# Empty steps, pinned evacuations and two moved units in a gated hybrid decoder layer

## The chip, the cores and the metric

The kernel runs on one core of one Trainium2 chip. The core has a TensorE (PE, matmuls; its weight loads are shown apart as PEld), a VectorE (DVE), a ScalarE (ACT), a GpSimd (POOL) and a SyncE (SP); each works off its own queue in order, and they wait for each other by semaphores. The metric is the device time of one execution in microseconds; of several runs the median is taken.

## The reference

One decoder layer on 256 tokens of width 2048, in float32 (shapes and small helpers left out):

```
h = rmsnorm(x, pre_norm_g)
proj = h @ w_in                       # 2048 x 18448
a_q, a_k, a_v, a_g, a_lr, b_q, b_k, b_v, b_g, m_a, m_b = split(proj)
gk  = log_sigmoid(a_lr @ gla_gk_w2 + gla_gk_b) / 16
o_a = gla_chunked(a_q, a_k, a_v, gk)  # gated linear attention, 4 heads
y_a = (rmsnorm(o_a) * silu(a_g)) @ w_branch_a
o_b = diff_attention(b_q, b_k, b_v, lam)   # softmax - lam * softmax, 16 heads
y_b = (rmsnorm(o_b) * (1 - lam_init) * silu(b_g)) @ w_branch_b
merged = sigmoid(m_a) * y_a + sigmoid(m_b) * y_b
out = x + rmsnorm(merged @ w_out, post_norm_g)
```

## The kernel before

**Weights stream, in units.** All products with the weight matrices are made in units of 128 x 1024 weights. For each unit ScalarE copies the raw weights to a rounded `hi` (line 314, in the sets 273), VectorE subtracts to get `lo` (315, in the sets 274), and TensorE multiplies `hi` with both parts of the other operand and `lo` with the first part. A streamed unit of the v, ag, m, y and o weights is 12 matmuls of 512 columns or fewer (line 480), one of the dq and dk weights 16 (lines 501 and 503). `raw`, `hi` and `lo` have three buffers each; a raw buffer holds two units and is loaded on SP's queue (line 293).

**Sets.** Seven further pieces of the product (`SETS`: the heads' dv and bg, and most merge gates) are made by a seven-product block scheme (`PRODUCTS`) instead of eight. Each set has 28 units of 6 matmuls (line 673). Some of its weights are combined by adding transfers on POOL's queue into `chain` tiles (lines 217 and 218), some by VectorE (231, 236), and one product reads plain weights through a `raw` buffer (267).

**One written order.** `schedule()` lists all units of the streams and the sets in the order in which TensorE takes them. `mixed(n, keys)` spreads the next n set units evenly among the units of those keys, `alone(n)` puts n set units in a row. `take(key)` hands out the next unit; it also writes the copies of units up to `AHEAD` = 4 ahead.

**Side work as generators.** Everything else is written by generators in the list `tasks`: the linear attention's scores (`gla_scores`) and outputs (`gla_out`), the splits of q and k of a pair of heads (`diff_split`), the differential attention (`diff_attention`), fetches, and the last joining of the branches (`joined`, `turned`, `turn`). `pump(n)` steps the first n tasks once, up to their next `yield`; it is called after units of the streams and after every second set unit. `tc.issue_after(latest[0])` orders the TensorE instructions of a step behind the latest matmul written; instructions of the other engines have no such bound, and the scheduler that fills the queues may place them earlier when their inputs are ready. `tc.keep_in_program_order` pins an instruction to its written place against that. Flags in `done` order the tasks among themselves: `diff_scores` of a pair is written only when its `split` flag is set, and a pair's weighing only when its set is done.

**The places that the change touches.**

- `gla_out(hf, gates)`: for two heads the products with the values (462), the norm (901 to 904), the gated product into `ua` on VectorE (907), then a `yield`; then for four columns the transpositions of `ua` (916), their evacuation by `split_out` (513 on ScalarE, 514 on VectorE) and stores. The first half runs during ag2, where `fast[0]` is set and `pump` is called after every unit.
- `diff_split`: copies and differences for a pair's q2, kh and kl (954 to 959). `diff_heads` puts it at the head of `tasks` after a pair's four channel groups.
- `diff_attention`: per head scores (978, 979, 983, 989), weights (995 to 999), transposition (1004), weighing with the values (1010 to 1012), norm and gated product (1020 to 1027), and per pair of heads transpositions (1055) and `split_out`.
- `turn(g)`: for each quarter g of the columns eight transpositions of the merged tile (1175), then, one or two steps later, two evacuations to `mh` and `ml` by `split_out`. `mh` and `ml` are the operands of the last product, o0 to o3. The quarters 0 to 2 are turned during y12 and y13, quarter 3 during o0.
- `fetch_a`: fetches the eight `oah` and `oal` tiles during m12 and m13, pinned on SP's queue; y00 to y03 use them.

Of the kernel before, what the change touches and what calls it, by code (L numbers as in the profile page):

```python
# [10 lines left out]
AF = mybir.ActivationFunctionType  # L11
# [19 lines left out]
def chunk_plan():  # L31

    plan = []
    at = 0
    for g, n in enumerate(VG):
        if g == 0:
            plan.append(("v0", "two", "w_in", [(6144, RANK), (2048, 2 * n - RANK)]))
            at = 2 * n - RANK
        elif g > 1:
            plan.append((f"v{g}", "tok", "w_in", [(2048 + at, n)]))  # L40
            at += n
    for hf in range(2):
        for name, base in (("k", 1024), ("q", 0)):
            for c in range(4):
                plan.append((f"{name}{hf}{c}", "chan", "w_in", [(base + 512 * hf + P * c, P)]))
    for g in range(4):
        plan.append((f"ag{g}", "tok", "w_in", [(4096 + 512 * g, 512)]))
    o = 6144 + RANK

    def heads(g):  # L50
        plan.append((f"dv{g}", "tok", "w_in", [(o + 4096 + 512 * g, 512)]))
        plan.append((f"bg{g}", "tok", "w_in", [(o + 6144 + 512 * g, 512)]))
        for pair in range(2):
            for n, name in enumerate(("dq", "dk")):
                for c in (2 * pair, 2 * pair + 1):
                    plan.append((f"{name}{g}{c}", "chan", "w_in", [(o + 2048 * n + 512 * g + P * c, P)]))

    def gate(br, g):
        plan.append((f"m{br}{g}", "tok", "w_in", [(o + 8192 + 2048 * br + 512 * g, 512)]))

    def branch(br, g):
        plan.append((f"y{br}{g}", "tok", ("w_branch_a", "w_branch_b")[br], [(512 * g, 512)]))

    for g in range(4):
        heads(g)
    for br, g in ((1, 2), (1, 3), (1, 0), (1, 1), (0, 0), (0, 1), (0, 2), (0, 3)):
        gate(br, g)
    for br in range(2):
        for g in range(4):
            branch(br, g)  # L70
    for g in range(4):
        plan.append((f"o{g}", "tok", "w_out", [(512 * g, 512)]))
    return plan
# [6 lines left out]
def schedule():  # L80

    kinds = {key: kind for key, kind, _, _ in chunk_plan()}
    steps = []
    blocks = [(i, n) for i in range(len(SETS)) for n in range(SLOTS * 4)]

    def regular(*keys):
        steps.extend((key, n) for key in keys for n in range(units(kinds[key])))

    def mixed(n, *keys):
        at = len(steps)  # L90
        regular(*keys)
        r = steps[at:]
        del steps[at:]
        for i, step in enumerate(r):
            steps.extend(blocks[: (i + 1) * n // len(r) - i * n // len(r)])
            del blocks[: (i + 1) * n // len(r) - i * n // len(r)]
            steps.append(step)

    def channels(g):
        return [key for key in kinds if key[:2] in ("dq", "dk") and key[2] == str(g)]  # L100

    order = [key for key, _, _, _ in chunk_plan()]
    def alone(n):
        steps.extend(blocks[:n])
        del blocks[:n]

    regular(*order[: order.index("v4")])
    mixed(SLOTS * 4, *order[order.index("v4") : order.index("ag0")])
    regular("ag0", "ag1")
    mixed(5, "ag2")  # L110
    mixed(8, "ag3")
    mixed(15, *channels(0))
    mixed(19, *channels(1))
    mixed(20, *channels(2))
    mixed(20, *channels(3))
    mixed(18, "m12", "m13")
    mixed(43, *(f"y0{g}" for g in range(4)))
    alone(4)
    mixed(16, "y10", "y11")
    regular("y12", "y13", *(f"o{g}" for g in range(4)))  # L120
    assert not blocks
    return steps
# [28 lines left out]
def hybrid_kernel(ctx: ExitStack, tc, xt, xn, preg, postg, w, w2, gkb, glag, lamv, diffg, ident_d, causal_d, lmask_d, out):  # L151
    nc = tc.nc
    pe, act, dve, pool, sp = nc.tensor, nc.scalar, nc.vector, nc.gpsimd, nc.sync
# [298 lines left out]
    fast = [False]  # L452
# [56 lines left out]
        act.activation(t, bank, AF.Tanh, scale=half_rstd[:, b : b + 1])  # L509
        dve.scalar_tensor_tensor(out=dst, in0=t, scalar=1.0, in1=bank, op0=ALU.add, op1=ALU.mult)  # L510

    def split_out(bank, hi, lo, gain):
        act.activation(hi, bank, AF.Copy, scale=gain)
        dve.scalar_tensor_tensor(out=lo, in0=bank, scalar=gain, in1=f32(hi), op0=ALU.mult, op1=ALU.subtract)


# [253 lines left out]
    for g, n in enumerate(VG[2:]):  # L770
        banks = token_major(f"v{g + 2}", n, x_ops, 2)
# [114 lines left out]
    def gla_out(hf, gates):  # L886
        og = []
        while f"scores{hf}" not in done:
            yield
        fetch_values(2 * hf + 1)  # L890
        for h in range(2):
            (ah, al), xh_, xl_ = att[hf], vh[2 * hf + h], vl[2 * hf + h]
            banks = [ps("bg"), ps("bg")]
            trio = lambda i, b: ((ah[:, i, h, :], xh_[:, b, :]), (ah[:, i, h, :], xl_[:, b, :]), (al[:, i, h, :], xh_[:, b, :]))
            product(banks[0], trio(0, 0), True, True)
            product(banks[1], trio(2, 0), True, False)
            product(banks[1], trio(1, 1), False, True)
            ssq = sm([P, 2], "gssq")
            junk = sm([P, 512], "junk", BF16, bufs=1)
            for b in range(2):  # L900
                act.activation(junk, banks[b], AF.Square, accum_out=ssq[:, b : b + 1])
            dve.scalar_tensor_tensor(out=ssq, in0=ssq, scalar=1.0 / 512.0, in1=gla_eps, op0=ALU.mult, op1=ALU.add)
            rsqrt(ssq, ssq)
            dve.tensor_tensor(out=ssq, in0=ssq, in1=half_rstd, op=ALU.mult)
            o = gates[h]
            for b in range(2):
                dve.scalar_tensor_tensor(out=o[:, b, :], in0=banks[b], scalar=ssq[:, b : b + 1], in1=o[:, b, :], op0=ALU.mult, op1=ALU.mult)
            og.append(o)
            yield
        for j in range(4):  # L910
            if j % 2 == 0:
                oah[2 * hf + j // 2], oal[2 * hf + j // 2] = u([P, 2, 2, S], "oah", F32R), u([P, 2, 2, S], "oal", F32R)
            bank = ps("bg")
            for h in range(2):
                for b in range(2):
                    pe.transpose(bank[:, P * (2 * h + b) : P * (2 * h + b) + P], og[h][:, b, P * j : P * j + P], ident)
            i = 2 * hf + j // 2
            hi = oah[i][:, j % 2].rearrange("p h t -> p (h t)")
            lo = oal[i][:, j % 2].rearrange("p h t -> p (h t)")
            split_out(bank, hi, lo, glag_s[:, j : j + 1])  # L920
            if j % 2:
                pool.dma_start(oah_far[i], f32(oah[i]))
                pool.dma_start(oal_far[i], f32(oal[i]))
                yield
        done.add(f"out{hf}")
# [7 lines left out]
    for g in range(4):  # L933
# [3 lines left out]
        banks = token_major(f"ag{g}", 512, x_ops)  # L937
# [11 lines left out]
    obl_far = [away([P, 4, S], "obl_far") for _ in range(4)]  # L949

    def diff_split(g, pair, tq, tk, q2, kh, kl):
        for m in range(2):
            own, other = slice(64 * m, 64 * m + 64), slice(64 - 64 * m, P - 64 * m)
            act.activation(q2[own, m], tq[own], AF.Copy)
            dve.tensor_tensor(out=q2[other, m], in0=tq[own], in1=f32(q2[own, m]), op=ALU.subtract)
            act.activation(kh[own, m], tk[own], AF.Copy)
            act.activation(kh[other, m], tk[own], AF.Copy)
            dve.tensor_tensor(out=kl[own, m], in0=tk[own], in1=f32(kh[own, m]), op=ALU.subtract)
            pool.memset(f32(kl[other, m]), 0.0)
        yield  # L960
        yield
        done.add(f"split{g}{pair}")
        yield
# [169 lines left out]
    for g in (2, 3):  # L1133
        banks = token_major(f"m1{g}", 512, x_ops, 2)
# [4 lines left out]
    for g in range(4):  # L1139
        if g == 3:  # L1140
            tasks.append(fetch_b())
        banks = token_major(f"y0{g}", 512, a_ops)
# [24 lines left out]
    def turn(g):  # L1167

        banks = []
        for i in range(2):  # L1170
            bank = ps("bg")
            for j in range(2):
                for b in range(2):
                    c = P * (2 * i + j)
                    pe.transpose(bank[:, P * (2 * j + b) : P * (2 * j + b) + P], both[g][:, b, c : c + P], ident)  # L1175
            banks.append(bank)
        yield
        if g < 3:
            yield
        for i in range(2):  # L1180
            hi = mh[g][:, 2 * i : 2 * i + 2, :].rearrange("p a t -> p (a t)")
            lo = ml[g][:, 2 * i : 2 * i + 2, :].rearrange("p a t -> p (a t)")
            split_out(banks[i], hi, lo, 0.5)

    def joined(g):
        yield from first_part(g)
# [13 lines left out]
    for g in range(4):  # L1200
        banks = token_major(f"y1{g}", 512, b_ops, 4)
# [59 lines left out]
    for g in range(3):  # L1261
        banks = token_major(f"o{g}", 512, m_ops)
# [3 lines left out]
    bank = ps("mm")  # L1266
# [8 lines left out]
    for c in range(2):  # L1275
        bank = ps("mm")
        for kt in range(KT):
            lo = 512 * (kt % 2) + 256 * c
# [68 lines left out]
```

## Time and profile before

| | |
|---|---|
| Three runs | 1111.54, 1114.25, 1114.8 us; median 1114.25 |
| The profiled execution | 1111.27 us |
| Its span, first to last instruction | 1109.5 us |
| VectorE, ScalarE busy | 866.6 us (78%), 702.6 us (63%) |
| HBM read, written | 253.64 MB, 24.12 MB; 250 GB/s over the span |
| Mean granted clock of TensorE | 0.998 |

A row of a timeline gives start and duration in us, engine, line, operation, the tiles (out<-in), shapes and count, and in brackets the idle time of the engine before it with what ended it. Rows that follow each other with the same line and form are merged (x8). A row of waits gives the instruction that waited, what released it, total us, how often, and the longest. "SPq" is the queue of SP, and its rows are issues of transfers.

### The profile page before, as it was taken

The page shows a single profiled execution, that of the slowest core. Times are in us where ns is not written, and L with a number is a line of the kernel's source. Part 1 is how long each engine was busy: PE and PEld are TensorE (multiplying, and loading weights), DVE is VectorE, ACT ScalarE, POOL GpSimd, SP SyncE. Part 2 cuts the span into 40 slices and gives each one's busy share as a digit, 9 for nine tenths or more (in the row PEclk, how much of TensorE's full clock was granted, in tenths as well). Part 3 has the DMA queues.
Part 4 walks back from the last instruction along what each step waited for, and adds up shares of the span by engine and source line. Part 5 has one row for each costly group of instructions (what it writes and reads, how often), then busy time and mean ns, then how long its engine had stood idle before and what let it go on. Part 6 is the DMA issues. An engine that isn't in the chain of part 4 may idle for free.

```text
span 1109.5 us, 15212 instructions
## 1 busy us (share of the span) xinstructions
PE 1091.8 (98%) x5530; PEld 938.6 (85%) x5530; DVE 866.6 (78%) x1203; ACT 702.6 (63%) x1031; POOL 167.6 (15%) x253
## 2 busy tenths in 40 slices
PE   9999999999999999999999999999999999999996
PEld 8999888888788888888888888887888888878886
DVE  6787779997878988869888898877777696585454
ACT  7877455654656667777877877756566565544441
POOL 0112102010301202202231222221111210000000
PEclk9999999999999999999999999999999999999999
DMA  8889875757889668988898968998787993587552
GB/s 310 272 321 316 235 250 211 283 186 267 249 286 301 214 244 216 238 239 218 264 245 247 279 204 261 261 330 297 224 238 253 316 346 139 204 327 298 195 190 77
DMA packets 59403, 278.75 MB, mean 251 GB/s; under 512 B 7296, under 2 KB 8064, under 8 KB 42944
## 3 DMA queue, kind: packets, MB, share of 16 engines
q1 hardware_dynamic: 31088, 177.10, 43.7%
q0 software_dynamic: 27520, 99.63, 34.1%
q10 hardware_dynamic: 720, 1.06, 0.3%
q8 instruction: 43, 0.70, 0.3%
q14 instruction: 32, 0.26, 0.1%
HBM read 253.64 MB, written 24.12 MB: 250 GB/s over the span
## 4 chain that ended last, share of the span: by engine, by line
PE 45%; issue 3%; DMA 2%; DVE 2%; ACT 1%; POOL 0%; DVEq 0%; POOLq 0%; ACTq 0%
PE mm L480 22%; PE set L673 13%; PE mm L501 5%; PE mm L503 2%; DMA raw_o<-in_w_dram 1%; DMA raw_s<-in_w_dram 1%; DVE lo L315 1%; PE mm L462 0%; ACT hi L314 0%; DVE lo L274 0%; PE bg L978 0%; PE bg L979 0%; PE bg L1004 0%; PE bg L1175 0%; ACT hi L273 0%
## 5 line engine op out<-in xcount | busy, mean ns | idle before, releaser
L273 ACT ACTIVATE hi<-chain 128x1024 fp32r<-128x1024 f32 x168 | 177.1, 1058 | 116.6 <-PE mm L480 47.4
L274 DVE TENSOR_TENSOR lo<-chain,hi 128x1024 fp32r<-128x1024 f32 x168 | 204.5, 1222 | 59.0 <-ACT hi L273 58.4
L501 PE MATMUL mm<-xs,hi 128*128 128x512 f32 x768 | 197.8, 390 | 1.8 <-ACT hi L314 1.8
L501 PEld LDWEIGHTS mm<-xs,hi 128*128 128x128 f32 x768 | 143.3, 188 | 30.3 <-ACT hi L314 2.6
L480 PE MATMUL mm<-hi,xs 128*128 128x512 f32 (+2 forms) x640 | 151.3, 376 | 1.2 <-ACT hi L314 1.2
L480 PEld LDWEIGHTS mm<-hi,xs 128*128 128x128 f32 x640 | 118.8, 188 | 16.9 <-ACT hi L314 1.8
L673 PE MATMUL set<-hi,square 128*128 128x512 f32 x448 | 121.8, 393 | 0.5 <-ACT hi L273 0.5
L503 PEld LDWEIGHTS mm<-xs,lo 128*128 128x128 f32 x768 | 104.8, 190 | 7.5
L503 PE MATMUL mm<-xs,lo 128*128 128x256 f32 x768 | 107.3, 282 | 0.0
L217 POOL DMA_DIRECT2D chain<-in_w_dram x72 | 62.9, 873 | 273.7 <-DVE lo L274 150.4
L315 DVE TENSOR_TENSOR lo<-raw_y,hi 128x1024 fp32r<-128x1024 f32 x64 | 78.1, 1223 | 30.1 <-ACT hi L314 30.1
L314 ACT ACTIVATE hi<-raw_y 128x1024 fp32r<-128x1024 f32 x64 | 67.6, 1060 | 46.5 <-PE mm L480 27.9
L673 PEld LDWEIGHTS set<-hi,square 128*128 128x128 f32 x448 | 81.6, 188 | 15.4 <-ACT hi L273 0.7
L673 PE MATMUL set<-hi,xs 128*128 128x512 f32 x336 | 91.3, 393 | 1.0 <-ACT hi L273 1.0
L480 PE MATMUL mm<-lo,xs 128*128 128x512 f32 (+2 forms) x320 | 81.8, 373 | 0.0
L673 PEld LDWEIGHTS set<-hi,xs 128*128 128x128 f32 x336 | 61.1, 189 | 11.8 <-ACT hi L273 1.4
L673 PE MATMUL set<-lo,square 128*128 128x512 f32 x224 | 69.2, 390 | 0.2 <-DVE lo L274 0.2
L480 PEld LDWEIGHTS mm<-lo,xs 128*128 128x128 f32 x320 | 59.8, 188 | 8.1 <-DVE lo L315 0.3
L314 ACT ACTIVATE hi<-raw_ag 128x1024 fp32r<-128x1024 f32 x32 | 33.9, 1060 | 30.6 <-PE mm L480 16.7
L315 DVE TENSOR_TENSOR lo<-raw_o,hi 128x1024 fp32r<-128x1024 f32 x25 | 30.6, 1225 | 28.3 <-ACT hi L314 28.2
L673 PE MATMUL set<-lo,xs 128*128 128x512 f32 x168 | 52.0, 391 | 0.1
L480 PE MATMUL mm<-hi,obh 128*128 128x512 f32 x128 | 50.2, 392 | 1.7 <-ACT hi L314 1.7
(270 smaller groups left out, 2081.6 us busy)
## 6 DMA issues: line engine op xcount, KB each, us to landing
chain<-in_w_dram POOLq DMA_DIRECT2D x128, 512.0 KB, 8.1
raw_y<-in_w_dram SPq DMA_DIRECT2D x32, 1024.0 KB, 7.7
raw_ag<-in_w_dram SPq DMA_DIRECT2D x16, 1024.0 KB, 5.0
raw_dq<-in_w_dram SPq DMA_DIRECT2D x16, 1024.0 KB, 7.7
raw_dk<-in_w_dram SPq DMA_DIRECT2D x16, 1024.0 KB, 7.0
raw_o<-in_w_dram SPq DMA_DIRECT2D x16, 1024.0 KB, 4.9
raw_v<-in_w_dram SPq DMA_DIRECT2D x14, 832.0 KB, 5.8
raw_k<-in_w_dram SPq DMA_DIRECT2D x8, 1024.0 KB, 7.1
```

The source lines that it names most:

```text
L217: return pool.dma_start(dst, src, accum_op=ALU.add)
L273: act.activation(hi_t, raw, AF.Copy)
L274: dve.tensor_tensor(out=lo_t, in0=raw, in1=f32(hi_t), op=ALU.subtract)
L314: act.activation(hi_t[:, a:b], r, AF.Copy)
L315: dve.tensor_tensor(out=lo_t[:, a:b], in0=r, in1=f32(hi_t[:, a:b]), op=ALU.subtract)
L480: i = pe.matmul(banks[g][b][:, :n], a[part][:, P * b : P * b + P], w[:, c : c + n], start=first, stop=last)
L501: i = pe.matmul(o, hi[:, c], x_pair(kt), start=kt == 0, stop=kt == KT - 1)
L503: i = pe.matmul(o[:, :S], lo[:, c], x_ops(kt)[0], start=False, stop=False)
L673: i = pe.matmul(bank, a[part], wt[:, 512 * j : 512 * j + 512], start=go, stop=end, skip_group_check=not first)
```

## The change

It has four parts.

1. `schedule()`: 16 set units instead of 18 are mixed into m12 and m13, and 18 instead of 16 into y10 and y11. All set units in between stand two places earlier in the sets' own order against the streams.
2. `gla_out`: one empty step ahead of the transpositions where `fast[0]` is set.
3. `diff_split`: one empty step ahead of its first instruction.
4. `turn`: the second empty step ahead of the evacuations of quarters 0 to 2 goes, and their ScalarE evacuations are pinned by `tc.keep_in_program_order`.

```diff
@@ schedule
-    mixed(18, "m12", "m13")
+    mixed(16, "m12", "m13")
     mixed(43, *(f"y0{g}" for g in range(4)))
     alone(4)
-    mixed(16, "y10", "y11")
+    mixed(18, "y10", "y11")
@@ split_out
-    def split_out(bank, hi, lo, gain):
-        act.activation(hi, bank, AF.Copy, scale=gain)
+    def split_out(bank, hi, lo, gain, pinned=False):
+        i = act.activation(hi, bank, AF.Copy, scale=gain)
+        if pinned:
+            tc.keep_in_program_order(i)
         dve.scalar_tensor_tensor(out=lo, in0=bank, scalar=gain, in1=f32(hi), op0=ALU.mult, op1=ALU.subtract)
@@ gla_out
             og.append(o)
             yield
+        if fast[0]:
+            yield
         for j in range(4):
@@ diff_split
     def diff_split(g, pair, tq, tk, q2, kh, kl):
+        yield
         for m in range(2):
@@ turn
         yield
-        if g < 3:
-            yield
         for i in range(2):
...
-            split_out(banks[i], hi, lo, 0.5)
+            split_out(banks[i], hi, lo, 0.5, g < 3)
```

## The prediction

> **What bounds the kernel now.** I read the page first (busy times, granted clock), then the waits of TensorE, then the stretches of time around each of those waits.
>
> ```profile
> PE 1091.8 (98%) x5530; PEld 938.6 (85%) x5530; DVE 866.6 (78%) x1203; ACT 702.6 (63%) x1031; POOL 167.6 (15%) x253
> PEclk9999999999999999999999999999999999999999
> ```
>
> The waits of TensorE (us in total, times, longest):
>
> ```profile
> PE mm L480 <- ACT hi L314: 2.8, 3, 1.7
> PE mm L501 <- ACT hi L314: 1.8, 2, 1.5
> PE set L673 <- ACT hi L273: 1.5, 2, 1.0
> PE bg L916 <- DVE ua L907: 1.2, 1, 1.2
> PE bg L395 <- DVE ones L392: 1.0, 1, 1.0
> PE mm L462 <- DVE keep L315: 0.4, 1, 0.4
> PE bg L1004 <- DVE prob L999: 0.4, 1, 0.4
> PE set L673 <- DVE lo L274: 0.2, 1, 0.2
> ```
>
> TensorE is busy for 98% of the span at a full clock, and no edit takes a matmul away. What can go is its idle time: the eight rows sum to 9.3 us. The start (L395, and the two small L480 waits) and the last tiles (L462) are not touched. The rest has four places, and each part of the change sits beside one of them. The profiled execution took 1111.27 us (span 1109.5 and 1.8 around it), 3.0 below the median of 1114.25; I sum against the profiled one and carry the difference to the median.
>
> "Step" below is one call of `take` (one unit of weights), counted through `schedule()` and the generators' yields; "turn" is one call of `pump`.
>
> **Part 1, the empty step in `gla_out`.** Only the first half's call runs while `fast[0]` is set, in ag2.
>
> ```profile
> 284.20 1.07 PE L673 MATMUL set<-hi,xs 128*128 128x512 f32 x4
> 285.11 0.62 PE L673 MATMUL set<-lo,xs 128*128 128x512 f32 x2
> ...
> 293.05 0.38 PE L916 MATMUL bg<-ident,ua 128*128 128x128 f32 x2
> ...
> 293.77 1.41 DVE L907 SCALAR_TENSOR_TENSOR ua<-bg,gssq,ua 128x512 f32<-128x512 f32 x2
> 294.58 0.66 PE L916 MATMUL bg<-ident,ua 128*128 128x128 f32 x4 [1.15 <-DVE ua L907]
> ```
>
> The third transposition comes 1.53 us after the first instead of 0.22, a loss of 1.31, because VectorE's products L907 end at 295.18 (the first halfway). With the empty step the transpositions are written after the next turn, which lies one set unit later: six matmuls at 0.227 (284.20 to the sixth's successor), 1.36 us. The third would then come at 293.27 + 1.36 = 294.63, after the first product and 0.55 ahead of the second's end. Bounds: gain 0.26, if a transposition must wait for the second product, to 1.31; I take 1.1, because the row shows TensorE doing three more transpositions before it needs that product. The four stores of this half on POOL's queue and the second half's scores each move one turn later; hiding them is the rest of ag2 and ag3, and by the count the second `gla_out` still starts at the same step.
>
> **Part 2, the pinned evacuation in `turn`.**
>
> ```profile
> 976.53 1.07 ACT L314 ACTIVATE hi<-raw_y 128x1024 fp32r<-128x1024 f32 x1 [1.66 <-PE mm L480]
> 986.03 1.08 ACT L513 ACTIVATE mh<-bg 128x512 fp32r<-128x512 f32 x2 [8.44 <-PE bg L1175]
> 987.00 2.95 ACT L314 ACTIVATE hi<-raw_y 128x1024 fp32r<-128x1024 f32 x3
> ...
> 985.40 1.03 PE L1175 MATMUL bg<-ident,mgate 128*128 128x128 f32 x8
> ...
> 988.12 0.50 PE L480 MATMUL mm<-hi,obh 128*128 128x512 f32 x1 [1.68 <-ACT hi L314]
> ...
> 993.70 1.03 PE L1175 MATMUL bg<-ident,mgate 128*128 128x128 f32 x8
> 994.49 0.48 PE L480 MATMUL mm<-hi,obh 128*128 128x512 f32 x1
> ```
>
> ScalarE's queue holds the first turned evacuation (L513) ahead of three weight copies (L314). It stands there 8.44 us until TensorE reaches the transpositions; then TensorE has no weights. From the transpositions to the next matmul are 2.72 us here and 0.79 at the next pair: a loss of 1.93. `tc.keep_in_program_order` pins L513 behind the copies written before it. `take` writes copies up to `AHEAD` = 4 units ahead, so the copies of y13's first units come first, and when TensorE reaches the transpositions it has its weights. Its place itself comes one turn earlier for three quarters; the transpositions do not move. Queued behind it on ScalarE are copies for five steps on (2.7 us each), and the first user of `mh` is o0, eight steps after the first transpositions: that is the cover, and without it the wait would be one of these evacuations, 1.1 us. Bounds: 0 (the pin holds it nowhere that matters) to 1.93; I take 1.93.
>
> **Part 3, the empty step in `diff_split`.** It issues no matmul and no transfer; what it moves is ScalarE, VectorE and POOL work (six copies of 0.63, four differences of about 0.7 and two memsets a pair, by the rows below) and, through the later "done" mark, all of the attention.
>
> ```profile
> 377.13 1.27 ACT L954 ACTIVATE q<-dq 64x512 fp32r<-64x512 f32 x2
> ...
> 386.44 1.10 POOL L959 MEMSET kl<- 64x512 f32 x2
> ...
> 386.83 0.42 DVE L1091 TENSOR_TENSOR dk<-dk,rstd_bc 128x256 f32<-128x256 f32 x1
> ...
> 393.39 1.23 DVE L236 TENSOR_TENSOR chain<-chain,raw_s 128x1024 f32<-128x1024 f32 x1 [1.73 <-DMA raw_s<-in_w_dram]
> ...
> 398.87 0.42 DVE L1091 TENSOR_TENSOR dk<-dk,rstd_bc 128x256 f32<-128x256 f32 x1
> ...
> 399.32 0.63 ACT L956 ACTIVATE kh<-dk 64x512 fp32r<-64x512 f32 x1 [3.78 <-DVE dk L1091]
> ...
> 400.34 0.67 DVE L958 TENSOR_TENSOR kl<-dk,kh 64x512 fp32r<-64x512 f32 x1
> ...
> 402.38 2.12 PE L501 MATMUL mm<-xs,hi 128*128 128x512 f32 x8 [1.49 <-ACT hi L314]
> ...
> 493.91 0.49 ACT L989 ACTIVATE prob<-prob,mx,score_scale 128x128 f32<-128x128 f32 x1 [2.42 <-DVE mx L984]
> ...
> 509.06 0.50 ACT L989 ACTIVATE prob<-prob,mx,score_scale 128x128 f32<-128x128 f32 x1 [3.52 <-DVE mx L984]
> ...
> 698.70 0.33 PE L1004 MATMUL bg<-ident,prob 128*128 128x128 f32 x1 [0.42 <-DVE prob L999]
> ```
>
> The first split is written where step 163 begins, near 399; its q part ran at 377 and its memset at 386. So ScalarE's order follows readiness, and an empty step alone does not push a split behind the weight copies. The 1.49 of the first pair comes from VectorE: L1091 is late behind a product that waited for a load (1.73). That load is not moved, so I leave 1.49. The other waits in this stretch (0.3 of L501, 0.5 of L673, 0.2 and 0.4, from the rows of waits, 1.4 in all) are exponentials or weights late behind VectorE. They depend on where a head's scores fall. Counted, heads follow each other by 12 and 7 steps in turn before, and by 9 steps after (7 and 5 for the last two): the narrow interval is wider, so I take 0.6 for 1.4. Against it, six of eight splits now share a turn with a head's weighing and scores, and the last attention pair ends at step 312 instead of 307, its transpositions one set unit (1.36) after its weighing; I add 0.4. Sum 2.9 to 2.5, gain 0.4. Bounds: gain 2.9, to a loss with every one of eight pairs stalling as the first does, 8 x 1.49 - 2.9 = 9.0.
>
> The Trainium skill (GPSIMD Engine Reference, 1 Specifications) says that GpSimd's SBUF interfaces are shared with VectorE and contend with its instructions of two SBUF inputs. By that rule moving the memsets into crowded turns would cost, and rival (e) below would be the case. The trace does not agree: L1091 (two SBUF inputs) took 0.42 beside the memset and 0.42 without it.
>
> **Part 4, two set units from m12/m13 to y10/y11.** The number of units is the same; m13 ends and y00 starts two units earlier, and sets 4 to 6 shift against y0.
>
> ```profile
> 722.99 0.33 SPq L267 DMA_DIRECT2D raw_s<-in_w_dram  x1
> ...
> 736.97 1.06 ACT L273 ACTIVATE hi<-raw_s 128x1024 fp32r<-128x1024 f32 x1 [0.75 <-PE set L673]
> ...
> 739.23 1.06 ACT L314 ACTIVATE hi<-raw_m 128x1024 fp32r<-128x1024 f32 x1 [1.20 <-PE mm L480]
> 740.33 1.23 DVE L315 TENSOR_TENSOR lo<-raw_m,hi 128x1024 fp32r<-128x1024 f32 x1 [1.04 <-ACT hi L314]
> ...
> 741.58 0.33 SPq L267 DMA_DIRECT2D raw_s<-in_w_dram  x1
> ...
> 749.51 1.06 ACT L273 ACTIVATE hi<-raw_s 128x1024 fp32r<-128x1024 f32 x1 [2.88 <-DMA raw_s<-in_w_dram]
> ...
> 750.62 1.19 PE L673 MATMUL set<-hi,xs 128*128 128x512 f32 x4 [0.99 <-ACT hi L273]
> ```
>
> This wait is one of buffers: `raw` has three, and the load for set 4's p2 (units 2 and 3) takes the one that m13's last unit frees, three steps ahead of its use. From that unit's copy to the matmul are 11.4 us; TensorE had 10.4 us of work. After the change I count the p2 load six steps ahead, but y00's second load then takes a buffer freed three steps ahead of its use (steps 318 and 321), with 10.0 us of matmuls between. So the wait changes its owner: up to 0.4 more if the load again takes 7.9, 0.99 less if it lands 2 us sooner. I take 0. The refills and SP loads of the two units move along with them. Ahead of p2's first load (issued 722.99, used 736.97, so about 6 us early at 7.9 a load) SP's queue holds the eight `oah` fetches of `fetch_a`, whose tiles come free as the attention ends, now five steps (some 10 us) later: up to 4 us late if the loads stay behind the fetches, nothing if they are issued first. I take nothing, since the queues are filled by readiness, as the early split at 377 shows; the 4 stays a bound.
>
> **The sum.** 1.93 + 1.1 + 0.4 + 0 = 3.4 us less: 1107.8 for the profiled execution, 1110.8 on the median, 0.31% faster.
>
> **Rivals.** (a) *The attention gives it back.* Splits crowd with scores, and three or four of the pairs stall by 1.49: 3.5 x 1.49 - 2.9 = 2.3 lost against 3.0 won, 1113.5. For it: VectorE at 78% is late wherever a wait is seen. Against: of eight splits one did this before.
> (b) *Every named wait goes*: 1.93 + 1.31 + 2.9 + 0.99 = 7.1, 1107.1. Against: the first split's cause is a load.
> (c) *The pin does not do what it says* (ScalarE still takes the evacuation early, as unpinned work is taken 22 us early at 377): 1.93 stays, 1112.7.
> (d) *Slower.* Splits and exponentials of the same turn stand in ScalarE's queue, waiting for VectorE, ahead of weight copies at all eight pairs: 11.9 - 2.9 - 3.0 = 6.0 lost, 1120.3. It decides from n x 1.49 > 2.9 + 3.0 + 3.3, seven of eight pairs; fewer only eat the gain.
> (e) *The memsets hold VectorE.* 1.10 a pair, all of it late on VectorE and on to TensorE: 8.8 lost against 3.4 won, 1119.6. Against: the two L1091 rows.
>
> **Chances.** About 0.3% (3.3 us) is what a measurement of this kernel can tell from no change. Forecast 0.47 (own range 1109 to 1112.5, two thirds of it below 1110.9), (a) 0.21, (b) 0.13, (c) 0.08, (d) 0.09, (e) 0.02. Faster: 0.31 + 0.13 and a little of (a), 0.45. Slower: (d), (e) and the edge of (a), 0.12. Same: 0.43. For 8 in 10 the range takes in the forecast, (b) and (c), and (a) up to five pairs (1115.8); it leaves out (d), (e) and the edges: 1106.5 to 1116.
>
> **What would show it.** In the profile after: no wait of L480 longer than 0.8 near 985, and the four pairs of L513 on `mh` with no idle time near 8.44 before them; no wait of L916 over 0.4; the L501 wait of the first split still there; in y00 a wait of an L480 copy for `raw_y` in place of the L673 one for `raw_s`. The sum is wrong if idle time of TensorE between 363 and 745 exceeds 6 us, or if that of the page falls by less than 2 us while the first two waits are gone.

## The result, and the profile after

The changed kernel took 1115.2 us (median of 22 runs), the kernel before 1112.22 us (22 runs beside them). The ratio is 1.0026, with a 95% interval of 1.0015 to 1.0038: slower by 0.15 to 0.38%, against a forecast of 0.31% faster. The time lies inside the range of the prediction, the sign is the other one. The 22 runs also put the kernel before 2.0 us below the 1114.25 that the prediction started from, which was the median of three.

The page of the changed kernel, the two rows that were shown of before:

```profile
PE 1093.1 (98%) x5530; PEld 939.2 (84%) x5530; DVE 866.9 (78%) x1203; ACT 704.0 (63%) x1031; POOL 167.2 (15%) x253
PEclk9999999999999999999999999999999999999999
```

TensorE is busy 1.3 us longer (1093.1 against 1091.8) with the same 5530 instructions; the clock row is too coarse to say why (the mean granted clock is 0.996 against 0.998). The span is 1111.8 us against 1109.5. The waits of TensorE, in the order of before (instruction, releaser, total us, how often, longest); lines behind an edit are up to 5 higher than before, since the change adds lines:

```profile
PE bg L1060 <- DVE ogb L1032: 3.5, 1, 3.5
PE mm L501 <- ACT hi L314: 2.6, 2, 1.6
PE mm L480 <- ACT hi L314: 2.0, 2, 1.4
PE bg L395 <- DVE ones L392: 1.1, 1, 1.1
PE mm L480 <- DVE lo L315: 0.8, 1, 0.8
PE mm L503 <- DVE lo L315: 0.6, 1, 0.6
PE set L675 <- ACT hi L273: 0.4, 1, 0.4
```

The rows sum to 11.0 us against 9.3; with the 1.3 us more of busy time that makes 3.0 more, against 2.3 in the span, and 0.7 of it I do not assign. The wait of the linear attention's transpositions (1.15) is gone, and so is the one of 1.7 behind the late evacuation. A new row stands on top: the transpositions of the last attention pair wait 3.47 us for `ogb`, the tile of the normed and gated product. TensorE's timeline there:

```profile
732.77 0.39 PE L1017 MATMUL bg<-dv,wt 128*128 128x128 f32 x2
...
734.38 0.38 PE L1060 MATMUL bg<-ident,ogb 128*128 128x128 f32 x2
734.52 2.07 PE L480 MATMUL mm<-hi,xs 128*128 128x512 f32 x8
736.43 0.84 PE L480 MATMUL mm<-lo,xs 128*128 128x512 f32 x3
740.74 0.33 PE L1060 MATMUL bg<-ident,ogb 128*128 128x128 f32 x1 [3.47 <-DVE ogb L1032]
...
741.17 1.28 PE L675 MATMUL set<-hi,square 128*128 128x512 f32 x4
742.24 1.06 PE L675 MATMUL set<-lo,square 128*128 128x512 f32 x2
743.09 3.12 PE L480 MATMUL mm<-hi,xs 128*128 128x512 f32 x8
...
746.98 1.09 PE L675 MATMUL set<-hi,square 128*128 128x512 f32 x4
```

And VectorE's, which shows what `ogb` stood behind:

```profile
725.09 1.22 DVE L315 TENSOR_TENSOR lo<-raw_m,hi 128x1024 fp32r<-128x1024 f32 x1
...
730.45 1.23 DVE L315 TENSOR_TENSOR lo<-raw_m,hi 128x1024 fp32r<-128x1024 f32 x1 [0.59 <-ACT hi L314]
734.60 1.23 DVE L236 TENSOR_TENSOR chain<-chain,raw_s 128x1024 f32<-128x1024 f32 x1 [2.93 <-DMA raw_s<-in_w_dram]
735.74 1.22 DVE L274 TENSOR_TENSOR lo<-chain,hi 128x1024 fp32r<-128x1024 f32 x1
736.88 1.22 DVE L236 TENSOR_TENSOR chain<-chain,raw_s 128x1024 f32<-128x1024 f32 x1
738.01 1.22 DVE L315 TENSOR_TENSOR lo<-raw_m,hi 128x1024 fp32r<-128x1024 f32 x1
739.15 0.15 DVE L1028 SCALAR_TENSOR_TENSOR de<-dssq,de 128x2 f32<-128x2 f32 x1
740.13 0.16 DVE L1030 TENSOR_TENSOR de<-de,half_rstd 128x2 f32<-128x2 f32 x1 [0.83 <-POOL de L407]
740.33 0.61 DVE L1032 SCALAR_TENSOR_TENSOR ogb<-bg,de,ub 128x128 f32<-128x128 f32 x2
```

The pair is weighed by 733 us, but its norm (L1028 to L1032) is the fifth in VectorE's queue. At the head stands the addition L236 of set 4's p2, which waits 2.93 us for `raw_s` (issued at 726.33 us, as shown below, and 8.2 us on its way). Between the first two transpositions and the last two TensorE has the streamed unit's matmuls, from 734.52 to 737.27 us, and then nothing. What a reader can take from the same view of before, which the prediction did not quote:

```profile
721.22 0.61 DVE L1027 SCALAR_TENSOR_TENSOR ogb<-bg,de,ub 128x128 f32<-128x128 f32 x2
...
729.89 1.22 DVE L236 TENSOR_TENSOR chain<-chain,raw_s 128x1024 f32<-128x1024 f32 x1 [2.67 <-DMA raw_s<-in_w_dram]
```

This addition waited for its load before too, for 2.67 us, and it cost nothing because the last pair's `ogb` had been made 8.67 us earlier.

The wait is not all. Three stretches of the changed kernel behind it (stretch, its length, busy time and count of the five engines, granted clock, DMA share, GB/s):

```profile
741.00:743.00 2.00, 2.00 (x9) 1.67 (x8) 2.00 (x3) 1.21 (x2) 0.56 (x1) 0.77 0.70 246
743.00:745.00 2.00, 2.00 (x6) 1.54 (x6) 1.75 (x2) 0.54 (x1) 1.08 (x3) 0.50 0.92 365
745.00:747.00 2.00, 2.00 (x10) 1.61 (x9) 0.00 (x0) 0.75 (x1) 0.00 (x0) 0.88 0.86 211
```

The granted clock halves. The set unit and the streamed unit from 741.17 to 746.98 take 5.81 us; the same pair of units takes 4.22 where the clock stayed (736.98 to 741.20 in the run `e3_split` below). So the place costs 3.47 of idle time and 1.6 of slow clock, 5.1 us in all.

### The profile page after: what moved, and what is told of

Its sections match the earlier page's. It is cut to its first block, busy times and chain, and to the rows that moved or that the text cites. A ratio compares the mean times of both kernels' runs of the same rounds, so it can differ in the third digit from the quotient of the medians.

```text
span 1111.8 us, 15224 instructions
## 1 busy us (share of the span) xinstructions
PE 1093.1 (98%) x5530; PEld 939.2 (84%) x5530; DVE 866.9 (78%) x1203; ACT 704.0 (63%) x1031; POOL 167.2 (15%) x253
## 4 chain that ended last, share of the span: by engine, by line
PE 88%; DMA 5%; DVE 3%; issue 2%; ACT 1%; POOL 0%; DVEq 0%; POOLq 0%; SPq 0%; ACTq 0%
PE mm L480 37%; PE set L675 22%; PE mm L501 14%; PE mm L503 7%; DMA raw_s<-in_w_dram 3%; PE bg L480 2%; DMA raw_y<-in_w_dram 2%; DVE lo L315 1%; PE bg L844 1%; PE mm L462 1%; DVE lo L274 1%; PE bg L462 1%; PE bg L983 1%; PE bg L984 1%; DMA raw_dk<-in_w_dram 1%
## 5 line engine op out<-in xcount | busy, mean ns | idle before, releaser
L501 PE MATMUL mm<-xs,hi 128*128 128x512 f32 x768 | 197.7, 390 | 2.6 <-ACT hi L314 2.6
L501 PEld LDWEIGHTS mm<-xs,hi 128*128 128x128 f32 x768 | 143.4, 188 | 31.4 <-ACT hi L314 3.6
L480 PE MATMUL mm<-hi,xs 128*128 128x512 f32 (+2 forms) x640 | 151.8, 377 | 0.6 <-ACT hi L314 0.6
L480 PEld LDWEIGHTS mm<-hi,xs 128*128 128x128 f32 x640 | 119.8, 189 | 16.6 <-ACT hi L314 0.9
L503 PEld LDWEIGHTS mm<-xs,lo 128*128 128x128 f32 x768 | 104.7, 190 | 8.6 <-DVE lo L315 1.3
L503 PE MATMUL mm<-xs,lo 128*128 128x256 f32 x768 | 107.5, 283 | 0.6 <-DVE lo L315 0.6
L217 POOL DMA_DIRECT2D chain<-in_w_dram x72 | 62.8, 872 | 282.3 <-DVE lo L274 164.6
L315 DVE TENSOR_TENSOR lo<-raw_y,hi 128x1024 fp32r<-128x1024 f32 x64 | 78.0, 1223 | 28.5 <-ACT hi L314 27.3
L480 PE MATMUL mm<-lo,xs 128*128 128x512 f32 (+2 forms) x320 | 82.2, 373 | 0.0
L480 PEld LDWEIGHTS mm<-lo,xs 128*128 128x128 f32 x320 | 59.8, 188 | 8.1 <-DVE lo L315 0.3
L218 POOL DMA_DIRECT2D chain<-in_w_dram x56 | 31.0, 560 | 147.8 <-DVE lo L274 137.8
L480 PE MATMUL mm<-hi,oah 128*128 128x512 f32 x128 | 49.9, 390 | 1.4 <-ACT hi L314 1.4
```

What stands on the lines that cost most here:

```text
L217: return pool.dma_start(dst, src, accum_op=ALU.add)
L218: return pool.dma_start(dst, src)
L315: dve.tensor_tensor(out=lo_t[:, a:b], in0=r, in1=f32(hi_t[:, a:b]), op=ALU.subtract)
L480: i = pe.matmul(banks[g][b][:, :n], a[part][:, P * b : P * b + P], w[:, c : c + n], start=first, stop=last)
L501: i = pe.matmul(o, hi[:, c], x_pair(kt), start=kt == 0, stop=kt == KT - 1)
L503: i = pe.matmul(o[:, :S], lo[:, c], x_ops(kt)[0], start=False, stop=False)
```

## The experiments

The first theory, T1, blamed the split's empty step alone, since it moves the end of the attention from step 307 to 312. Its rivals: R1, the moved set units; R2, that any shift of this order brings as much waiting as it removes. The first four runs make one part each.

**Part 1 alone.**

```diff
@@ gla_out
             yield
+        if fast[0]:
+            yield
```

> The kernel before with the empty step in gla_out alone. Theory T1 (the time of the whole change was lost by the last attention pair, which comes five steps later and has its norm caught on VectorE behind a weight split that waits for its load): this part has nothing to do with it, the wait of 1.15 us at the transpositions of the gated rows goes, 1.3 us less than before, ratio 0.999. Rival R2 (any shift of the order makes waits as large as it removes): the wait goes and others of 1 us or more take its place, ratio 1.000 or above.

Measured: 1110.5 us, ratio 0.998 (0.9969 to 0.9991). The wait of L916 is gone; y00's wait for `raw_s` is 2.1 instead of 1.0, so the waits that can be seen explain little of the gain. T1 agrees. R2 has the new wait that it asked for (1.1 us more in y00), but not the time.

**Part 2 alone.**

```diff
@@ split_out, turn
...
+        if pinned:
+            tc.keep_in_program_order(i)
...
-        if g < 3:
-            yield
...
-            split_out(banks[i], hi, lo, 0.5)
+            split_out(banks[i], hi, lo, 0.5, g < 3)
```

> The kernel before with the pinned evacuations and the step taken out of second_part alone. T1: the idle time of 8.4 us ahead of ScalarE's late evacuation and TensorE's wait behind it (1.7 us) go, some 0.8 to 1 us of wait comes back in y13, where lo stands on VectorE behind the bank products: about 1 us less than before, ratio 0.999. R2: nothing gained, ratio 1.000 or above.

Measured: 1111.07 us, ratio 0.9986 (0.9976 to 0.9996). The wait of 1.7 is gone and one of 0.8 for `lo` has come, as expected.

**Part 3 alone.**

```diff
@@ diff_split
+        yield
         for m in range(2):
```

> The kernel before with the empty step in diff_split alone. T1: the transpositions of the last attention pair come at step 312 instead of 307, and wait 3 to 4 us for ogb; the granted clock is below 0.8 in the few us behind that wait; 4 to 5.5 us more than before, ratio 1.004 to 1.005. Rival R1 (the two set units that were moved cause it, as they put the load of raw_s later): the transpositions wait under 1 us here, and the time is within 1 us of before.

Measured: 1110.88 us, ratio 0.9991 (0.9977 to 1.0005). T1 is refuted: the last pair is as late as in the whole change, and nothing waits for it. VectorE's timeline of this run, and then TensorE's:

```profile
727.92 1.22 DVE L236 TENSOR_TENSOR chain<-chain,raw_s 128x1024 f32<-128x1024 f32 x1 [0.29 <-DMA raw_s<-in_w_dram]
...
735.04 0.16 DVE L1024 SCALAR_TENSOR_TENSOR de<-dssq,de 128x2 f32<-128x2 f32 x1
...
736.23 0.61 DVE L1028 SCALAR_TENSOR_TENSOR ogb<-bg,de,ub 128x128 f32<-128x128 f32 x2
```

```profile
736.31 0.91 PE L1056 MATMUL bg<-ident,ogb 128*128 128x128 f32 x4
736.98 1.18 PE L673 MATMUL set<-hi,square 128*128 128x512 f32 x4
...
741.20 1.07 PE L673 MATMUL set<-hi,square 128*128 128x512 f32 x4
```

The addition has its load 6.7 us earlier here (727.92 instead of 734.60 us), and the norm is not held up by it.

**Part 4 alone.**

```diff
@@ schedule
-    mixed(18, "m12", "m13")
+    mixed(16, "m12", "m13")
...
-    mixed(16, "y10", "y11")
+    mixed(18, "y10", "y11")
```

> The kernel before with the two set units moved alone. T1: attention ends at step 307 as before, and its last pair's transpositions don't wait; the wait of 1 us for raw_s becomes one of 1.0 to 1.4 us for raw_y in y00; 0 to 0.4 us more than before, ratio 1.000. R1: the transpositions of the last attention pair wait 3 us or more and the clock drops behind them, 4 to 5.5 us more than before, ratio 1.004 to 1.005.

Measured: 1111.13 us, ratio 0.9987 (0.9975 to 0.9998). R1 is refuted too: the moved units alone put the load of `raw_s` at 730.44 us (722.99 before), and nothing waits for it (the queues of SP and VectorE in this run):

```profile
730.44 8.86 SPq L267 DMA_DIRECT2D raw_s<-in_w_dram  x2
...
736.59 1.22 DVE L236 TENSOR_TENSOR chain<-chain,raw_s 128x1024 f32<-128x1024 f32 x1
```

VectorE comes to the addition only at 736.59 us here, and the load is there. No part is slower than before, three of the four are faster, and the whole is slower: it is a meeting of parts. That made theory T3 (the norm comes late by the split's step, and the addition ahead of it waits for a load that comes late by the moved units); the next four runs take one part out of the whole, or bend it.

**All but the split's step**, and **all but the moved units**: the diffs of part 3 and of part 4, undone in the changed kernel.

> The changed kernel without the empty step in diff_split. The four parts alone each cost nothing, so T1 and R1 as they stood have fallen. Theory T3 (the loss is a meeting of two parts: the split's step puts the last attention pair's norm five steps later, and the moved units put the load of raw_s later; only with both does the norm stand on VectorE behind an addition that waits for raw_s): without the split's step the norm is ahead of that addition again; no wait of the last transpositions, no slow clock, the gains of the other parts stay, 2.5 to 4 us below before, ratio 0.9965 to 0.998. Rival R2 (each shift of the order brings some wait, and the sum of four is what was measured): 1 us or more above before, with waits that none of the single runs shows.

> The changed kernel with the two set units where they were. T3: raw_s is loaded as early as in the run of the split's step alone, VectorE waits under 1 us for it, the last transpositions wait under 0.5 us, no slow clock; 2 to 3.5 us below before, ratio 0.997 to 0.998. R2: at or above before.

Measured: without the split's step 1110.05 us, ratio 0.9976 (0.9963 to 0.9988). Without the moved units 1107.92 us, ratio 0.9958 (0.9941 to 0.9974). Neither shows a wait of the last transpositions, and the granted clock is 1.00 in both from 720 to 755 us. T3 expected both, and the second to be a little less fast than it is (0.997 to 0.998; it has six runs only); R2 is refuted, since it had no way to 0.42% below before with three of the four parts in.

**More work ahead of the transpositions.**

```diff
@@ diff_attention, in the changed kernel
+            if pair and not new and not last:
+                yield
+                yield
             if pair:
                 bank = ps("bg")
```

> The changed kernel with two empty steps more ahead of the last attention pair's transpositions, so that TensorE has one more square unit and its product (some 4 us) in front of them. T3: VectorE still waits about 3 us for raw_s and the norm is as late as it was, but the transpositions no longer wait over 1 us; what TensorE can wait for instead is the lo of the unit put ahead, which stands behind the same addition, by at most 1.5 us; the clock stays above 0.95; 3 to 5 us below the changed kernel, ratio to before 0.998 to 1.000. If VectorE's wait for raw_s stops TensorE whatever stands next (rival R3), a wait of 3 us stays at the unit's own matmuls, with the slow clock, and the time is within 1 us of the changed kernel.

Measured: 1113.57 us, ratio 1.0007 (0.9996 to 1.0018), about 2 us below the changed kernel and not the 3 to 5 that T3 gave. The transpositions wait no more, yet VectorE is still held by loads of `raw_s`, now by the second one (in this run's timelines of VectorE and of TensorE):

```profile
742.71 1.22 DVE L315 TENSOR_TENSOR lo<-raw_y,hi 128x1024 fp32r<-128x1024 f32 x1
746.81 1.23 DVE L236 TENSOR_TENSOR chain<-chain,raw_s 128x1024 f32<-128x1024 f32 x1 [2.89 <-DMA raw_s<-in_w_dram]
747.96 1.22 DVE L274 TENSOR_TENSOR lo<-raw_s,hi 128x1024 fp32r<-128x1024 f32 x1
```

```profile
749.23 0.73 PE L675 MATMUL set<-lo,xs 128*128 128x512 f32 x2 [2.66 <-DVE lo L274]
...
754.14 1.09 PE L675 MATMUL set<-hi,xs 128*128 128x512 f32 x4
```

Rival R3 was partly right: what waits is whatever VectorE makes next for TensorE. A wait of 2.66 came back some 8 us later, with a slow clock of its own (0.54 from 750 to 752 us).

**One unit moved instead of two.**

```diff
@@ schedule, in the changed kernel
-    mixed(16, "m12", "m13")
+    mixed(17, "m12", "m13")
...
-    mixed(18, "y10", "y11")
+    mixed(17, "y10", "y11")
```

> The changed kernel with one set unit moved instead of two (17 and 17). T3: the load of raw_s comes some 1.4 to 2 us earlier than with two and the addition that waits for it stands four places ahead of the norm instead of being its near neighbour; VectorE's wait for raw_s 0.5 to 2 us, that of the last transpositions under 1 us, the clock stays; 2 to 4 us below the changed kernel, ratio to before 0.998 to 1.000. R2: still above before, ratio 1.002 or more.

Measured: 1109.41 us, ratio 0.997 (0.9959 to 0.9981), some 6 us below the changed kernel by the two ratios: more than expected, for one unit. SP's queue in the changed kernel and then in this one:

```profile
718.82 0.33 SPq L293 DMA_DIRECT2D raw_y<-in_w_dram  x1
726.33 13.25 SPq L267 DMA_DIRECT2D raw_s<-in_w_dram  x2
```

```profile
719.91 0.33 SPq L267 DMA_DIRECT2D raw_s<-in_w_dram  x1
727.42 0.33 SPq L293 DMA_DIRECT2D raw_y<-in_w_dram  x1
```

The second unit swaps two loads. With one unit moved, as with none, `raw_s` of set 4's p2 is issued ahead of y00's first `raw_y`. With two it comes behind it, and has to wait for the next raw buffer, which the L315 shown above at 725.09 gives free at 726.3. That is 6.4 us later, for a shift of one unit of 1.4 us. This run differs in one more point: the last two transpositions stand further back in TensorE's queue (740.51 and 740.91 us), so it does not separate the load's place from theirs. The next run does.

**The load's place alone.** One set unit is taken out of the mix with y00 to y03 and put ahead of it; the written places of the norm and of the last transpositions among their neighbours stay as in the changed kernel.

```diff
@@ schedule, in the changed kernel
     mixed(16, "m12", "m13")
-    mixed(43, *(f"y0{g}" for g in range(4)))
+    alone(1)
+    mixed(42, *(f"y0{g}" for g in range(4)))
```

> The changed kernel with one set unit taken from the y00 to y03 stretch and put ahead of it, so that the load of raw_s (set 4's p2) stands ahead of y00's first raw_y in SP's queue again, while the m stage keeps its 16 units and the split its step. T3, now with its place (the two moved units swap these two loads; raw_s then waits for the next raw buffer): raw_s is issued near 719 instead of 726.3 us and has landed before VectorE's addition, VectorE's wait for it falls from 2.9 to under 0.5 us, the last transpositions wait under 1 us, the clock stays at 1.00; 4 to 6 us below the changed kernel, ratio to before 0.996 to 0.998. If the place of the norm alone decides (rival R4), the transpositions wait 2 us or more here too, ratio 1.000 or above.

Measured: 1114.34 us, ratio 1.0014 (1.0000 to 1.0027). In the profile the mechanism came out as T3 said; the time is as R4 said. The timelines of SP, VectorE and TensorE in this run (lines are one higher than in the changed kernel):

```profile
718.74 0.33 SPq L268 DMA_DIRECT2D raw_s<-in_w_dram  x1
```

```profile
726.21 1.22 DVE L237 TENSOR_TENSOR chain<-chain,raw_s 128x1024 f32<-128x1024 f32 x1
```

```profile
737.83 0.33 PE L1061 MATMUL bg<-ident,ogb 128*128 128x128 f32 x1 [0.68 <-DVE ogb L1033]
...
748.82 0.61 PE L676 MATMUL set<-lo,xs 128*128 128x512 f32 x2
...
751.99 1.07 PE L676 MATMUL set<-hi,xs 128*128 128x512 f32 x4
...
756.15 0.50 PE L481 MATMUL mm<-hi,oah 128*128 128x512 f32 x1 [2.64 <-ACT hi L315]
```

The load is issued 7.6 us earlier, the addition no longer waits (2.93 to 0), and the transpositions wait 0.68 instead of 3.47. The clock is 1.00 from 720 to 755 us. In this execution rival R4 is refuted: with the load in time, the late pair does not make the 3.47. (With its load the addition itself moves up in VectorE's queue, to 726.21 us, so the run moves both.) But the next load is late now: TensorE waits 2.64 us at 753.5 us for y00's next weights, whose `raw_y` was issued at 746.2.

The profiled execution is the quickest of this kernel's twelve, which reach from 1110.18 to 1118.28 us, so it does not stand for the usual one. The granted clock that every run lists says more: it is 0.998 in the two quickest and 0.995 to 0.997 in the other ten. Averaged over all runs it is 0.9956 in the changed kernel, 0.9965 here and in `e8_late_pair`, and 0.9978 to 0.9985 in the nine other kernels tried. So on average an execution of this run does lose clock: from 0.998 to 0.9965 are 0.0015, of 1110 us 1.7 us (an estimate), as much as the slow stretch above cost. That it loses it behind the wait of 2.64 is likely, but no profile shows it, and the rest of the distance to the quickest run is open.

**What the split's step is worth, and the fastest version again.** The first is the kernel before with parts 1 and 2; the second repeats the changed kernel without the moved units.

> The kernel before with the step in gla_out and the pinned evacuations, without the split's step and without the moved units. If the split's step gains nothing of its own, this is as fast as the changed kernel without the units, ratio 0.9955 to 0.9970; from the waits that went in the two single runs (1.2 and 0.9 us) 0.9975 to 0.9985 is expected, and the split's step is then worth about 1 to 2 us.

> The changed kernel with the two set units where they were, once more, as the fastest version so far and with only six undisturbed runs: ratio to before 0.9950 to 0.9975 if the first measurement holds.

Measured: parts 1 and 2 1109.54 us, ratio 0.998 (0.9967 to 0.9994); with the split's step on top 1108.51 us, ratio 0.9967 (0.9955 to 0.9979), inside its expectation. The intervals of the two overlap, so a gain of the split's step on its own is not shown. The version without the moved units is the fastest of all, 0.33 to 0.42% below before in its two measurements, and beats both kernels.

## Why the prediction was wrong

**Part 1, right.** Forecast: 1.1 of the 1.31 at L916. The wait is gone in the profile after; alone, the part is 0.1 to 0.3% faster.

**Part 2, right in its mechanism, with twice the size.** No idle time stands ahead of the evacuations any more (8.44 us before), and the weights are copied first. ScalarE's and TensorE's timelines of the changed kernel:

```profile
989.04 2.01 ACT L314 ACTIVATE hi<-raw_y 128x1024 fp32r<-128x1024 f32 x2 [7.15 <-PE mm L480]
...
1001.01 1.06 ACT L513 ACTIVATE mh<-bg 128x512 fp32r<-128x512 f32 x2
```

```profile
992.20 0.39 PE L480 MATMUL mm<-hi,obl 128*128 128x512 f32 x1
993.36 1.19 PE L480 MATMUL mm<-lo,obh 128*128 128x512 f32 x4 [0.77 <-DVE lo L315]
```

The 7.15 us now ahead of the copies are a wait for their weights, although the bracket names TensorE: that `raw_y` was issued at 980.69 us and took 8.3 us to land. Before, a load issued at 975.92 us had landed after as many, near 984.2, and only the evacuation held the copies back until 987.00. What was late next is the `lo` of y13's first unit on VectorE (0.77). From the transpositions on, that takes 0.93 (992.20 to 993.36 us between two matmuls instead of 0.23), and of the gain of 1.93 that was forecast 1.0 is left; the part alone is 0.04 to 0.24% faster.

**Part 3, the step that failed.** The prediction saw that the last pair would end at step 312, its transpositions one unit behind its weighing, and charged 0.4 us. It looked only at what TensorE has to do in the meantime. On VectorE the norm of that pair came to stand behind the L236 that waits for `raw_s`, a wait of 2.67 us that the trace of before already had, at no cost then. Measured: 3.47 of wait and 1.6 of slow clock. The rest of the part: the first split's wait stayed (1.6 where 1.49 was left standing). The other waits of the attention did not fall from 1.4 to 0.6; the rows for L501 (2.6 less the 1.6), L503 and the set add up to 2.0. By the prediction's own sign, more than 6 us of TensorE idle between 363 and 745 us, the sum was wrong: 1.6, 2.0 and 3.5 make 7.1.

**Part 4, half right.** The wait in y00 changed its owner as counted, from `raw_s` (0.99) to `raw_y` (the 1.4 of the L480 row, at the edge of the 0.4 more that was allowed). But the prediction asked only when ScalarE copies set 4's p2 for TensorE (736.97 us, "about 6 us early"), not that VectorE's L236 reads the same load far sooner and was waiting for it already, and took nothing for the load behind SP's queue. The load did come later, by 3.3 us, not for the fetches that were suspected but for a raw buffer, since y00's load had gone ahead of it.

**The sum.** Forecast 3.4 us gained. Measured between the two medians: 3.0 lost. Parts 1 and 2 gained some 2.3 in the profile (1.3 and 1.0), and the place above lost 5.1, where the prediction had 0.4 for the late pair and 0 for the late load. Neither part costs this alone (`e3_split`, `e4_units`): only the two together do, and the prediction priced each part by itself and added. The profile of `e6_no_units`, which has the other three parts, says the same: its span is 7.0 us shorter than that of the changed kernel, and of that the `ogb` wait is 3.5, busy time 1.1 and the L480 waits on ScalarE 1.6. Rival (d) had the sign, but its splits and exponentials did not stall at each pair; its place, price and point of decision were others. By the prediction's bound of 0.3% the result is its "Same", which had 0.43; that is no merit of the sum, since the whole 95% interval lies on the slower side. That the time lies inside the range is luck as well: the starting point was 2.0 us too high, and the upper end had been set for rival (a), whose stalls did not come.

## What to carry to other kernels

Before moving work to a later place, read the queues of all engines there for waits that cost nothing now: a wait for a load on VectorE is free only as long as nothing urgent stands behind it. When two edits shift the same stretch, work out the order of the queue with both made, since the cost may belong to neither. And where loads share a ring of buffers, count which load takes the next one: a shift of one unit of 1.4 us moved a load by 6.4 us here.

## What was not expected of the hardware

An idle TensorE loses its clock for longer than the wait itself suggests. After 3.47 us of idle time the granted clock of the three stretches above (0.77, 0.50 and 0.88 over 2 us each) adds up to 0.46 + 1.00 + 0.24 = 1.7 us lost, that is 3.4 us at half clock. Read in stretches of half a microsecond it is one piece, from 742.08 to 745.50 us, and it began some 1.3 us after work had begun again. The Trainium skill (TensorE: Matmul & The Clock Gate, Part 1: The HAM clock gate) tells of such halving after an idle window of about 3.4 us, and of a like time to come back; the second figure agrees with the trace. The first does not hold as a lower limit here: in `e8_late_pair` 2.66 us of idle time sufficed, and the units from 749.23 to 754.14 took 4.91 us where the same ones took 3.17 (748.82 to 751.99 in `e11_raw_s_first`). In the latter run 2.64 us of idle time did not suffice, in this row of its stretches:

```profile
757.00:759.00 2.00, 2.00 (x10) 1.64 (x9) 2.00 (x3) 1.70 (x3) 0.00 (x0) 1.00 0.16 64
```

Two waits of one length, with and without the loss: the same page of the Trainium skill says that the window runs freely and does not start with the work, which would make it a matter of phase. The traces bear this out. In all 13 of them (one for each kernel here) the granted clock changes only on a grid of 3.41 us: the stretch at full clock ahead of the halving is 216 such steps long in the changed kernel and 218 in `e8_late_pair`, and each of these two halvings lasts one step. Where TensorE's idle time lies on this grid decides:

| Run | The wait | Most idle time in one step of the grid | Clock in the next step |
|---|---|---|---|
| `e8_late_pair` | 2.66 us | 2.50 us (746.73 to 750.15) | 0.50 |
| the changed kernel | 3.47 us | 2.07 us (738.67 to 742.08) | 0.50 |
| `e11_raw_s_first` | 2.64 us | 1.73 us (751.82 to 755.24) | 1.00 |
| `e1_gla` | 2.06 us | 1.22 us (747.39 to 750.80) | 1.00 |

At the end, where TensorE runs out of work, all 13 traces halve too, each behind the first step with 2.02 us of idle time or more. No step with 1.73 us or less was followed by a slow clock, the wait of 1.68 us of the kernel before included. So in these traces it took more than 1.73 and at most 2.02 us of idle time within one step. The grid lies otherwise in each execution: its first record stands 4.2 to 10.1 us behind the first instruction. One and the same wait can so cost the clock in one execution and not in the next.

The clock column has a blind spot at the start. Ahead of that first record it prints 1.00, but in `e1_gla`, where the record begins at 10.1 us, four matmuls of 416 columns took 1.59 us from 6.91 us on, and 0.92 us in the changed kernel at 6.35 us, where it begins at 4.8.
